# Rotated keys: one transpose per head pair and a copy to the other partitions; the last rows scaled into a tile of their own

## The chip, the cores and the metric

The kernel runs on one NeuronCore of a Trainium2 chip. The metric is device time in microseconds (us), as the median of several executions; lower is better. Five engines run their own instruction streams and wait for each other by semaphores: TensorE (PE, matrix products and transposes), VectorE (DVE), ScalarE (ACT), GpSimd (POOL) and SyncE (SP). SP issues only transfers (DMAs); ACT issues transfers between its activations, and a transfer that ACT has to wait with holds up the activations behind it.

## The reference

Two layers, each with three token mixers (a state-space scan, sliding-window attention, forgetting attention) fed by one input projection of the normalised stream, then gates, an output projection and a residual sum; at the end one RMS norm. The change touches the keys of the sliding-window mixer and the last norm:

```python
def rms_norm(x, w):
    xf = x.astype(jnp.float32)
    y = xf * lax.rsqrt(jnp.mean(xf * xf, axis=-1, keepdims=True) + NORM_EPS)
    return (y * w.astype(jnp.float32)).astype(x.dtype)

def rope(x, cos, sin):
    half = x.shape[-1] // 2
    x1, x2 = x[..., :half], x[..., half:]
    c, s = cos[None, :, None, :], sin[None, :, None, :]
    return jnp.concatenate([x1 * c - x2 * s, x2 * c + x1 * s], axis=-1)

def sliding_window_branch(q, k, v, z, sinks, cos, sin):
    ...
    q = rope(q.reshape(b, s, SWA_HEADS, HEAD_DIM), cos, sin)
    k = rope(k.reshape(b, s, SWA_KV_HEADS, HEAD_DIM), cos, sin)
    ...
    scores = jnp.einsum('bnqkgd,bnskd->bnkgqs', qb, kb).astype(jnp.float32) * (HEAD_DIM ** -0.5)
```

There are 256 tokens, a model width of 1024, 16 query heads and 4 key heads of 64 columns each. All is float32.

## The kernel before

**Products.** Each float32 product of the projections is made of three passes of a faster format: a weight piece `raw` arrives by a transfer (512 KB, L341, on SP), ACT writes its rounded part `hi` (L264), DVE the rest `lo` (L265), and PE runs hi·hi, hi·lo and lo·hi (L96). Six buffers each of `raw`, `hi` and `lo` go round: a transfer into a `raw` buffer waits until DVE has split what was in it, and ACT writes a `hi` buffer when PE has read the old one. The result of a projection stands in one of three PSUM buffers (`mm`), and the third projection after it waits until that buffer has been read.

**Order.** A planner with a clock of PE work (`pump`, `launch`, `drain`) decides at build time where the small steps of the mixers are put between the projections on PE. PE's order is kept as planned; for the other engines a scheduler orders the instructions, apart from the first three steps of layer 0, where all engines keep the planned order. Each engine then runs its list strictly in turn.

**Keys.** `u_bkv` (L476) projects the keys of 128 tokens (t = 0, 1), `rope` (L465) rotates them on DVE, and POOL adds the two halves of the rotation (L492). A score product takes queries of 64 partitions, and the queries `qT` (L522) hold two heads, one in partitions 0 to 63, the other in 64 to 127. The two heads use one key head, so that the keys are wanted in both halves. The kernel before writes each key head twice side by side (`kd`), and the transpose of that, 128x128, holds the head in both halves: four transposes on PE (L499, recorded as L100) and one activation (L500) for each t. `y.kT` holds the four heads, 256 tokens each. The first score products (`swa_quad`, L605, PE line L96 with `mx<-L,qt`) come after the first gate projection of that mixer (`u_z`, L773).

**Constants.** Ahead of the second L500 of layer 0, ACT issues the transfers of small constants of the layer (`layer_consts`, L408; they are recorded as L259): `vr`, four of `hb`, and two of `dsk`. Each `dsk` transfer brings 64x8 single elements of 4 bytes.

**Completion semaphores.** Transfers of SP and ACT use eight completion semaphores in turn, in the order in which the program has them (DMAHW0 to DMAHW7). A transfer whose semaphore was used by an earlier one that hasn't landed waits for it, on the engine that issues it.

**The end.** `out_end` (L993) adds the residual (L996, DVE), takes the sum of squares (L215, ACT), multiplies by the norm weight in place (L1001, DVE), and after the last columns works out the row factor (L1008, L226 on POOL, L228, L230) and scales the two halves of the row on DVE (L1011) and ACT (L1013), each followed by its transfer out. L1001 writes what L215 reads, and so comes after it.

Of the kernel before, what the change touches and what calls it, by code (L numbers as in the profile page):

```python
# [13 lines left out]
AF = mybir.ActivationFunctionType  # L14
ALU = mybir.AluOpType

P = 128
S = 256
D = 1024
# [6 lines left out]
D_K, D_Q, D_QK, D_G0, D_FOX, D_BDMA, D_BIAS = 6.0, 5.5, 2.0, 8.0, 0.0, 4.0, 2.0  # L26
# [17 lines left out]
def hybrid_trunk(  # L44
# [5 lines left out]
    nc = tc.nc  # L50
    x2 = x.flatten_outer_dims()
    out2 = out.flatten_outer_dims()
# [9 lines left out]
    def T(tag, shape, dtype=F32, bufs=None):  # L62
        count[0] += 1
        return sb.tile(shape, dtype, tag=tag, name=f"{tag}_{count[0]}",
                       bufs=bufs if bufs is not None else BUFS.get(tag, 1))
# [8 lines left out]
    def pmx():  # L74
        return PS("mx", 5)

    act = nc.scalar.activation
    stt = nc.vector.scalar_tensor_tensor
    tt = nc.vector.tensor_tensor
    ts = nc.vector.tensor_scalar  # L80
    gtt = nc.gpsimd.tensor_tensor
# [16 lines left out]
    def transpose(o, a, i):  # L98
        clock["t"] += 0.109
        nc.tensor.transpose(o, a, i)  # L100

    def launch(br, gen, delay=0.0):
        clock["n"] += 1
        waiting.append([clock["t"] + delay, clock["n"], br, gen, None])
# [24 lines left out]
    def pump(budget=BUDGET):  # L129
        t0 = clock["t"]  # L130
        while clock["t"] - t0 < budget:
            for m in sorted(waiting, key=lambda m: (m[0], m[1])):
                if ready(m):
                    enter(m)
                    break
            else:
                return
# [26 lines left out]
    ident = T("ident", [P, P])  # L164
# [47 lines left out]
    def sum_sq(xt, t, c, ss, n=256):  # L212

        junk = T("L2", [P, 512])
        act(junk[:, 0:n], xt[:, t, c:c + n], AF.Square, accum_out=ss)  # L215

    def row_var(ss, n):
        v = T("sm", [P, 8])
        nc.vector.tensor_reduce(v[:, 0:1], ss[:, 0:n], axis=mybir.AxisListType.X, op=ALU.add)
        ts(v[:, 0:1], v[:, 0:1], 1.0 / D, EPS, op0=ALU.mult, op1=ALU.add)  # L220
        return v
# [32 lines left out]
    def halves(ap):  # L254

        return ap.rearrange("p (a i) -> p a i", a=2)
# [142 lines left out]
    for l in range(L):  # L399
        y = Layer()  # L400
# [46 lines left out]
    def tok(ah, al, w, t, turn=True, mid=None, **kw):  # L447


        n = w.n  # L450
        p = pmm()
        b = in_turn if turn else lambda ap: ap
        if mid is None and n == 512:
            mid = pump
        dense(p[:, 0:n], lambda k: still(ah, t, k), lambda k: still(al, t, k), lambda k: b(w.hi(k)),
              lambda k: b(w.lo(k)), w, mid=mid, **kw)
        return ordered(p[:, 0:n]) if turn else p[:, 0:n]
# [7 lines left out]
    def rope(p, t):  # L465

        p4 = p.rearrange("p (h d) -> p h d", h=4)
        cos = bc(rope_sb[:, t, 0, :], 1, 4)
        a = T("L1", [P, 4, 64])
        tt(a, p4, cos, op=ALU.mult)  # L470
        b = T("L1", [P, 4, 64])
        tt(b[:, :, 0:32], p4[:, :, 32:64], bc(rope_sb[:, t, 1, 0:32], 1, 4), op=ALU.mult)
        tt(b[:, :, 32:64], p4[:, :, 0:32], bc(rope_sb[:, t, 1, 32:64], 1, 4), op=ALU.mult)  # L473
        return a, b

    def u_bkv(y, c0, t, after=None):  # L476

        def f(w):
            p = tok(y.hTh, y.hTl, w, t, turn=w.n == 512 or c0 > 0, after=after)
            if t == 0 and c0 == 0:  # L480
                kv = T("L8", [P, 2048])
                y.kT = kv[:, 0:1024].rearrange("p (h s) -> p h s", h=4)
                y.bv = kv[:, 1024:1536].rearrange("p (t c) -> p t c", t=2)
            if c0 > 0:
                act(halves(y.bv[:, t, :]), p, AF.Copy)
            elif w.n == 512:
                act(y.bv[:, t, :], p[:, 1, :], AF.Copy)
            if c0 == 0:
                a, b = rope(p if w.n == 256 else p[:, 0, :], t)
                kd = T("L2", [P, 4, 2, 64])  # L490
                for i in range(2):
                    gtt(kd[:, :, i, :], a, b, op=ALU.add)  # L492
                launch(1, rest(kd), D_K)
            pump()

        def rest(kd):
            pt = pmx()
            for h in range(4):
                transpose(pt[:, h * P:(h + 1) * P], kd[:, h, :, :].rearrange("p a b -> p (a b)"), ident)  # L499
            act(y.kT[:, :, t * P:(t + 1) * P], pt.rearrange("p (h s) -> p h s", h=4), AF.Copy)  # L500
            yield 0.0
        return f

    def u_bq(y, c0, t):
# [488 lines left out]
    def out_end(y, c, t, i, n, xo, p):  # L993
        sl = slice(c, c + n)
        with tc.high_priority():
            tt(halves(y.xn[:, t, sl]), p, halves(xo), op=ALU.add)  # L996
            sum_sq(y.xn, t, c, y.ss[t][:, i:i + 1], n)
            last = y.l + 1 == L
            nwb = fin["w"] if last else layers[y.l + 1].nwb
            if last:  # L1000
                stt(y.xn[:, t, sl], y.xn[:, t, sl], -0.5, nwb[:, sl], op0=ALU.mult, op1=ALU.mult)  # L1001
            else:
                nc.scalar.dma_start(xres[t * P:(t + 1) * P, sl], y.xn[:, t, sl])
            if i == 1:
                y.var[t] = row_var(y.ss[t], 2)
            if i == 2:
                v = y.var[t][:, 1:2]
                stt(v, y.ss[t][:, 2:3], 1.0 / D, y.var[t][:, 0:1], op0=ALU.mult, op1=ALU.add)  # L1008
                r = row_rsqrt2(v)
                if last:  # L1010
                    ts(y.xn[:, t, 0:512], y.xn[:, t, 0:512], r[:, 0:1], None, op0=ALU.mult)  # L1011
                    nc.sync.dma_start(out2[t * P:(t + 1) * P, 0:512], y.xn[:, t, 0:512])
                    act(y.xn[:, t, 512:D], y.xn[:, t, 512:D], AF.Copy, scale=r[:, 0:1])  # L1013
                    nc.scalar.dma_start(out2[t * P:(t + 1) * P, 512:D], y.xn[:, t, 512:D])
                else:
                    h = layers[y.l + 1].h[t] = T("L4", [P, D])
                    for j in range(2):
                        hs = slice(j * 512, (j + 1) * 512)
                        stt(h[:, hs], y.xn[:, t, hs], r[:, 0:1], nwb[:, hs], op0=ALU.mult, op1=ALU.mult)
        if i == 2 and not last:  # L1020
            launch(5 + t, hT(layers[y.l + 1], t), D_H[t])
        if i == 1:
            pump()

    fin = {}
# [23 lines left out]
    for y in layers:  # L1049
# [4 lines left out]
        def cols(c0, n=256):  # L1054
            return sub([(0, w[:, c0:c0 + n])], n)
# [27 lines left out]
        if l == 0:  # L1083
            k, v = cols(C_BK), cols(C_BV)
# [40 lines left out]
        o = [sub([(0, w_out[l, :, c:c + n])], n) for c, n in ((0, 256), (256, 512), (768, 256))]  # L1125
# [13 lines left out]
    with tc.manual_schedule(engines={ENG.PE, ENG.DVE, ENG.Activation, ENG.Pool}):  # L1139
# [5 lines left out]
        h = [T("L4", [P, D]) for _ in range(2)]  # L1145
# [76 lines left out]
```

## Time and profile before

| | us |
|---|---|
| runs (3) | 847.7, 848.38, 850.29 |
| median | 848.38 |
| span of the profiled execution, first to last instruction | 846.0 |
| PE busy in it | 833.7 |
| DVE, ACT, POOL busy | 642.3, 511.6, 105.7 |

The span leaves out what lies before the first instruction and after the last. The page says how long each engine was busy, which chain of work ended last, and which groups of instructions cost most; other views of the same execution list the instructions in order of time, the waits, the stretches, and the transfers with their time from issue to landing. In a row of the order of time stand its start, its length, engine, line, operation, output and inputs, shapes, and in brackets the idle time of the engine before it with what ended it; rows of equal instructions that overlap are merged, and the length is then that of all. A matmul's recorded length overlaps the next one's; the chain of waits gives what each adds.

### The profile page before, as it was taken

To read this page: it belongs to the slowest core of one execution; us is meant where nothing else is said; L and a number is where in the kernel's file an instruction comes from. 1 tells how busy PE (TensorE), PEld (TensorE's weight loads), DVE (VectorE), ACT (ScalarE), POOL (GpSimd) and SP (SyncE) were. 2 spreads that over 40 slices of the span, in tenths; PEclk is the share of its full clock that TensorE was granted. 3 is DMA by queue.
4 is the path that set the end of the run, shared out by engine and by line. 5 is a ranking of instruction groups with operands and counts; after the bars stand their busy time and mean duration, and the time that the engine had idled before them with its cause. 6 is when DMAs were issued, how large, how long until landed. Compare 5 with 4: busy or idle time off the path is not lost.

```text
span 846.0 us, 15985 instructions
## 1 busy us (share of the span) xinstructions
PE 833.7 (99%) x5964; PEld 763.4 (90%) x5964; DVE 642.3 (76%) x1403; ACT 511.6 (60%) x1004; POOL 105.7 (12%) x134
## 2 busy tenths in 40 slices
PE   8999999999999999999999999999999999999996
PEld 7989898998999998888989998899899999988896
DVE  5777997998776669656788879879968567785665
ACT  6466777665666667435555667776557667654442
POOL 6410100000140010210014001000003110121000
PEclk9999999999999999999999999999999999999999
DMA  9576565666465545748676465465755654576632
GB/s 303 160 226 197 180 199 163 197 212 184 143 188 177 181 145 189 230 147 292 206 237 218 144 204 157 145 200 182 239 172 176 174 175 152 161 236 211 212 100 76
DMA packets 126638, 158.43 MB, mean 187 GB/s; under 512 B 12784, under 2 KB 88224, under 8 KB 126560
## 3 DMA queue, kind: packets, MB, share of 16 engines
q1 hardware_dynamic: 109456, 140.79, 52.5%
q10 hardware_dynamic: 17056, 16.49, 6.3%
q8 instruction: 47, 0.77, 0.4%
q14 instruction: 31, 0.25, 0.1%
q0 software_dynamic: 48, 0.13, 0.0%
HBM read 155.22 MB, written 2.16 MB: 186 GB/s over the span
## 4 chain that ended last, share of the span: by engine, by line
PE 95%; DMA 3%; DVE 1%; ACT 0%; POOL 0%; issue 0%; SPq 0%; POOLq 0%; DVEq 0%
PE mm L96 82%; PE mx L96 9%; PE mx L100 4%; DMA raw<-in_w_in_dram 3%; DVE lo L265 0%; POOL lo L1154 0%; ACT hi L1153 0%; DVE L L470 0%; ACT L L1013 0%; DVE L L265 0%; ACT L L264 0%; POOLq L1218 0%; ACT L L215 0%; DVE L L996 0%; DVE L L1001 0%
## 5 line engine op out<-in xcount | busy, mean ns | idle before, releaser
L265 DVE TENSOR_TENSOR lo<-raw,hi 128x1024 fp32r<-128x1024 f32 x252 | 308.3, 1235 | 93.8 <-ACT hi L264 84.6
L96 PE MATMUL mm<-hi,L 128*128 128x512 f32 (+1 forms) x1344 | 373.9, 364 | 2.0 <-ACT hi L1153 1.5
L264 ACT ACTIVATE hi<-raw 128x1024 fp32r<-128x1024 f32 x252 | 263.4, 1056 | 93.5 <-PE mm L96 75.5
L96 PE MATMUL mm<-L,hi 128*128 128x256 f32 x1792 | 317.7, 278 | 0.7 <-DVE L L473 0.7
L96 PEld LDWEIGHTS mm<-L,hi 128*128 128x128 f32 x1792 | 277.7, 192 | 7.6 <-issue 3.3
L96 PEld LDWEIGHTS mm<-hi,L 128*128 128x128 f32 x1344 | 241.5, 190 | 32.5 <-issue 2.7
L96 PE MATMUL mm<-L,lo 128*128 128x256 f32 x896 | 246.4, 275 | 0.0
L96 PE MATMUL mm<-lo,L 128*128 128x512 f32 (+1 forms) x672 | 241.4, 361 | 0.6 <-POOL lo L1154 0.6
L96 PEld LDWEIGHTS mm<-L,lo 128*128 128x128 f32 x896 | 171.9, 192 | 0.2
L96 PEld LDWEIGHTS mm<-lo,L 128*128 128x128 f32 x672 | 127.3, 190 | 15.4 <-POOL lo L1154 0.8
L867 POOL TENSOR_SCALAR_AFFINE_SELECT bias<-bias 128x128 f32<-128x128 f32 x64 | 35.9, 597 | 407.5 <-DVE L L736 268.6
L561 ACT ACTIVATE pp<-pp,nm 128x128 f32<-128x128 f32 (+1 forms) x128 | 56.5, 443 | 13.5 <-DVE nm L555 13.5
L698 DVE SCALAR_TENSOR_TENSOR L<-L,vec,L 128x255 f32<-128x255 f32 (+2 forms) x96 | 46.3, 482 | 4.7 <-ACT L L695 3.4
L96 PE MATMUL mx<-L,L 128*64 128x128 f32 (+1 forms) x384 | 34.4, 314 | 0.0
L891 ACT ACTIVATE L<-L 128x512 f32<-128x512 f32 x24 | 15.1, 631 | 29.9 <-DVE L L890 29.7
L573 DVE TENSOR_SCALAR pp<-pp,rsum 128x128 f32<-128x128 f32 (+1 forms) x128 | 32.2, 316 | 0.5
L701 ACT ACTIVATE L<-L 128x256 f32<-128x256 f32 x32 | 13.3, 417 | 31.5 <-DVE L L698 25.9
L96 PEld LDWEIGHTS mx<-L,L 128*64 128x64 f32 x384 | 23.0, 136 | 9.4 <-ACT pp L561 1.3
L782 ACT ACTIVATE L<-mm 128x256 f32<-128x256 f32 x48 | 18.1, 378 | 20.8 <-PE mm L96 20.8
L590 ACT ACTIVATE L<-mx 128x512 f32<-128x512 f32 x48 | 27.0, 597 | 2.7 <-PE mx L100 2.5
L100 PE MATMUL mx<-ident,pp 128*128 128x128 f32 x192 | 26.3, 273 | 0.0
L555 DVE CUSTOM_DVE_ANT_0 pp<-mx,wmask,nsink 128x128 f32<-128x128 f32 x64 | 23.4, 412 | 1.5 <-PE mx L96 1.5
(173 smaller groups left out, 717.5 us busy)
## 6 DMA issues: line engine op xcount, KB each, us to landing
raw<-in_w_in_dram SPq DMA_DIRECT2D x200, 512.0 KB, 4.5
raw<-in_w_proj_dram SPq DMA_DIRECT2D x48, 512.0 KB, 5.5
raw<-in_w_out_dram SPq DMA_DIRECT2D x16, 512.0 KB, 4.6
L<-cumd ACTq DMA_DIRECT2D x8, 512.0 KB, 5.0
bias<-cumd ACTq DMA_DIRECT2D x16, 256.0 KB, 4.0
L<-in_gate_bias_dram ACTq DMA_DIRECT2D x12, 256.0 KB, 3.9
L<-in_x_dram SPq DMA_DIRECT2D x2, 512.0 KB, 4.9
nwb<-in_norm_w_dram SPq DMA_DIRECT2D x1, 512.0 KB, 5.3
```

The source lines that it names most:

```text
L96: nc.tensor.matmul(o, a, b, **kw)
L100: nc.tensor.transpose(o, a, i)
L264: keep(act)(hi, src, AF.Copy)
L265: keep(tt)(lo, src, hi.bitcast(F32), op=ALU.subtract)
L555: nc.vector.tensor_tensor_reduce(out=pp[:, i, sl], in0=score(p, i, b), in1=biases(p, i, b), scale=-0.125, scalar=1.0e30 if ns is None else ...
L561: act(pp[:, i, sl], pp[:, i, sl], AF.Exp, scale=-1.0, bias=nm[:, e:e + 1], accum_out=sums[:, e:e + 1])
L573: ts(pp[:, i, sl], pp[:, i, sl], rs[:, 2 * i + b:2 * i + b + 1], 0.5, op0=ALU.mult, op1=ALU.mult)
L590: act(pT, pt, AF.Copy)
L698: stt(a[:, s:S], x_[:, 0:S - s], y.vec[:, 16 * j + u:16 * j + u + 1], a[:, s:S], op0=ALU.mult, op1=ALU.add)
L782: act(halves(th), p, AF.Tanh, scale=0.5)
L867: nc.gpsimd.affine_select(out=bias[:, i, dst], in_=bias[:, i, src], compare_op=ALU.is_ge, fill=NEG, base=0, pattern=[[-1, P]], channel_mul ...
L891: act(g, g, AF.Tanh, scale=0.5)
```

## The change

For each t the keys are rotated into a tile `k` of four heads side by side, with one addition on POOL. Two transposes on PE, each of a pair of heads, give the even heads in partitions 0 to 63 and the odd ones in 64 to 127. Two activations of 64 partitions put them into `y.kT`. After t = 1 two transfers issued by ACT copy the even heads to partitions 64 to 127 and the odd ones to 0 to 63: 64 partitions, 2 heads, 256 tokens, 128 KB each. In the last layer the product with the norm weight goes into a new tile `fin["y"]` in place of `y.xn`, and the row factor and the transfers out work on that tile.

```diff
             if c0 == 0:
                 a, b = rope(p if w.n == 256 else p[:, 0, :], t)
-                kd = T("L2", [P, 4, 2, 64])
+                k = T("L1", [P, 4, 64])
+                gtt(k, a, b, op=ALU.add)
+                launch(1, rest(k.rearrange("p h d -> p (h d)")), D_K)
+            pump()
+
+        def rest(k):
+            pt = pmx()
+            for j in range(2):
+                transpose(pt[:, j * P:(j + 1) * P], k[:, j * P:(j + 1) * P], ident)
+            k2 = y.kT.rearrange("p (j i) s -> p j i s", i=2)
+            for i in range(2):
+                r = slice(64 * i, 64 * i + 64)
+                act(k2[r, :, i, t * P:(t + 1) * P], pt[r, 0:2 * P].rearrange("p (j s) -> p j s", j=2), AF.Copy)
+            yield 0.0
+            if t == 1:
                 for i in range(2):
-                    gtt(kd[:, :, i, :], a, b, op=ALU.add)
-                launch(1, rest(kd), D_K)
-            pump()
-
-        def rest(kd):
-            pt = pmx()
-            for h in range(4):
-                transpose(pt[:, h * P:(h + 1) * P], kd[:, h, :, :].rearrange("p a b -> p (a b)"), ident)
-            act(y.kT[:, :, t * P:(t + 1) * P], pt.rearrange("p (h s) -> p h s", h=4), AF.Copy)
-            yield 0.0
+                    nc.scalar.dma_start(k2[64 - 64 * i:128 - 64 * i, :, i, :], k2[64 * i:64 * i + 64, :, i, :])
...
             if last:
-                stt(y.xn[:, t, sl], y.xn[:, t, sl], -0.5, nwb[:, sl], op0=ALU.mult, op1=ALU.mult)
+                if i == 0 and t == 0:
+                    fin["y"] = T("L8", [P, 2, D])
+                stt(fin["y"][:, t, sl], y.xn[:, t, sl], -0.5, nwb[:, sl], op0=ALU.mult, op1=ALU.mult)
...
                 if last:
-                    ts(y.xn[:, t, 0:512], y.xn[:, t, 0:512], r[:, 0:1], None, op0=ALU.mult)
-                    nc.sync.dma_start(out2[t * P:(t + 1) * P, 0:512], y.xn[:, t, 0:512])
-                    act(y.xn[:, t, 512:D], y.xn[:, t, 512:D], AF.Copy, scale=r[:, 0:1])
-                    nc.scalar.dma_start(out2[t * P:(t + 1) * P, 512:D], y.xn[:, t, 512:D])
+                    o = fin["y"]
+                    ts(o[:, t, 0:512], o[:, t, 0:512], r[:, 0:1], None, op0=ALU.mult)
+                    nc.sync.dma_start(out2[t * P:(t + 1) * P, 0:512], o[:, t, 0:512])
+                    act(o[:, t, 512:D], o[:, t, 512:D], AF.Copy, scale=r[:, 0:1])
+                    nc.scalar.dma_start(out2[t * P:(t + 1) * P, 512:D], o[:, t, 512:D])
```

**How it moves instructions.** First ACT in layer 0, around the second step of the keys, where the constants are issued; `hi_491` and `hi_503` before (`hi_489` and `hi_501` after) are the last two pieces of the second query projection, which PE takes up at 39.76 us of the profile before. Before:

```order
L259 DMA hb_405<-in_a_log_dram 128x16
L259 DMA dsk_410<-in_d_skip_dram 64x8x1 x2
L500 ACTIVATE L_50_265<-mx_426 128x4x128
L264 ACTIVATE hi_491<-raw_319 128x1024
L264 ACTIVATE hi_503<-raw_325 128x1024
```

With the change:

```order
L259 DMA hb_402<-in_a_log_dram 128x16
L259 DMA dsk_407<-in_d_skip_dram 64x8x1 x2
L502 ACTIVATE L_50_265<-mx_423 64x2x128 x2
L506 DMA L_50_265<-L_50_265 64x2x256 x2
L264 ACTIVATE hi_489<-raw_317 128x1024
L264 ACTIVATE hi_501<-raw_323 128x1024
```

The two copies stand directly behind the two `dsk` transfers in ACT's list, and ahead of the two `hi` pieces.

Second SP in layer 0: the weight pieces issued from about 33 us on, with the semaphores that each waits for (DVE: the `raw` buffer must be split; a completion semaphore: an earlier transfer must have landed). The two copies take two completion semaphores in between, so that the pieces behind them get other ones. Before:

```order
L341 DMA raw_495<-in_w_in_dram 128x4x256 [waits DMAHW4_49,DMAHW2_49,DVE_49]
L341 DMA raw_507<-in_w_in_dram 128x4x256 [waits DMAHW7_49,DMAHW6_49,DVE_49]
L341 DMA raw_590<-in_w_in_dram 128x4x256 [waits DMAHW7_49,DMAHW0_49,DVE_49]
L341 DMA raw_596<-in_w_in_dram 128x4x256 [waits DMAHW1_49,DMAHW0_49,DVE_49]
L341 DMA raw_608<-in_w_in_dram 128x4x256 [waits DMAHW1_49,DVE_49]
L341 DMA raw_620<-in_w_in_dram 128x4x256 [waits DMAHW2_49,DVE_49]
```

With the change:

```order
L341 DMA raw_493<-in_w_in_dram 128x4x256 [waits DMAHW4_49,DMAHW2_49,DVE_49]
L341 DMA raw_505<-in_w_in_dram 128x4x256 [waits DMAHW7_49,DMAHW0_49,DVE_49]
L341 DMA raw_588<-in_w_in_dram 128x4x256 [waits DMAHW1_49,DVE_49]
L341 DMA raw_594<-in_w_in_dram 128x4x256 [waits DMAHW2_49,DVE_49]
L341 DMA raw_606<-in_w_in_dram 128x4x256 [waits DMAHW3_49,DVE_49]
L341 DMA raw_618<-in_w_in_dram 128x4x256 [waits DMAHW6_49,DMAHW4_49,DVE_49]
```

Semaphore 2 belongs to the first row in both. Before, the sixth row waited for it; with the change the fourth does, two transfers earlier.

Third DVE at the end, the last 256 columns of the second 128 rows, with what each instruction waits for. Before:

```order
L996 TENSOR_TENSOR L_1975_10131<-mm_10332,L_2007_10330 128x256 [waits PE_49]
L1001 SCALAR_TENSOR_TENSOR L_1975_10131<-L_1975_10131,nwb_9781 128x256 [waits Activation_49]
L1008 SCALAR_TENSOR_TENSOR sm_10327<-ss_10134,sm_10327 128x1
L228 SCALAR_TENSOR_TENSOR sm_10364<-sm_10362,sm_10327 128x1 [waits Pool_49]
```

With the change:

```order
L1001 TENSOR_TENSOR L_1975_10127<-mm_10329,L_2008_10327 128x256 [waits PE_49]
L1008 SCALAR_TENSOR_TENSOR L_1988_10203<-L_1975_10127,nwb_9777 128x256 [waits DVE_49]
L1015 SCALAR_TENSOR_TENSOR sm_10324<-ss_10130,sm_10324 128x1 [waits Activation_49]
L228 SCALAR_TENSOR_TENSOR sm_10361<-sm_10359,sm_10324 128x1 [waits Pool_49]
```

The product with the norm weight (L1001 before, L1008 now) no longer waits for ACT's sum of squares; the first step of the row factor does.

On PE nothing moves but the transposes of the keys, two in place of four at each of four places, and in layer 1 the next transposes a few products apart. In layer 1 ACT and DVE also split the 64-column piece of the small projection (128x8x32) two weight pieces earlier than before.

## The prediction

> **What bounds the kernel now.** First the page, then the waits of PE, then the chain of waits between 20 and 60 us, where the keys of layer 0 are made.
>
> ```profile
> PE 833.7 (99%) x5964; PEld 763.4 (90%) x5964; DVE 642.3 (76%) x1403; ACT 511.6 (60%) x1004; POOL 105.7 (12%) x134
> PE 95%; DMA 3%; DVE 1%; ACT 0%; POOL 0%; issue 0%; SPq 0%; POOLq 0%; DVEq 0%
> ```
>
> PE is busy for 99% of the span and is 95% of the chain: an edit is worth what it takes from PE's list, or from the few places where PE stands. The waits of PE from 30 to 840 us, the longest (in total, times, longest one):
>
> ```profile
> PE mm L96 <- DVE L L473: 0.7, 1, 0.7
> ```
>
> That one wait is what matters here. The chain (start, length, what):
>
> ```profile
> 25.74 0.44 PE mx L100 x4
> ...
> 28.77 0.44 PE mx L100 x4
> ...
> 36.82 15.02 DMA raw<-in_w_in_dram
> ...
> 55.40 2.95 PE mm L96 x24
> ```
>
> The two L100 rows are the key transposes of layer 0. Behind them the chain leaves PE: a weight piece that SP begins to issue at 36.82 takes 15.0 us to land, and PE goes on at 55.40 only after what hangs on it. Why 15 us is told by stretches and two groups of transfers:
>
> ```profile
> 36.00:40.00 4.00, 4.00 (x22) 3.52 (x21) 4.00 (x7) 1.81 (x3) 1.27 (x1) 1.00 0.05 0
> 40.00:44.00 4.00, 4.00 (x23) 3.50 (x22) 1.81 (x9) 1.15 (x4) 1.44 (x3) 1.00 0.04 0
> 44.00:46.00 2.00, 2.00 (x11) 1.76 (x10) 1.00 (x3) 1.06 (x1) 1.13 (x2) 1.00 0.56 183
> 46.00:50.00 4.00, 4.00 (x30) 3.68 (x29) 1.14 (x2) 1.07 (x1) 0.00 (x0) 1.00 1.09 360
> ```
>
> ```profile
> L259 ACTq DMA_DIRECT2D dsk<-in_d_skip_dram x2: 646/646/646, 31.5 to 32.2; - x2
> DMA to landing us min/median/max: 9.8/9.8/9.8
> ```
>
> ```profile
> L341 SPq DMA_DIRECT2D raw<-in_w_in_dram x1: 368/368/368, 33.7 to 33.7; - x1
> DMA to landing us min/median/max: 14.5/14.5/14.5
> ```
>
> The last two numbers of a stretch are the share of the DMA engines and GB/s. From 36 to 44 nothing but the single elements of `dsk` moves; the first landed 9.8 us after its issue, and the piece issued at 33.7, behind them, at 48.2. From 44 the backlog of pieces runs, at 360 GB/s from 46. The keys' copies are issued into this jam.
>
> The wait it causes, in order of time:
>
> ```profile
> 51.94 1.07 ACT L264 ACTIVATE hi<-raw 128x1024 fp32r<-128x1024 f32 x1 [0.45 <-DMA raw<-in_w_in_dram]
> 53.09 1.58 PE L96 MATMUL mx<-L,qt 64*128 64x128 f32 x16
> 53.40 1.21 DVE L265 TENSOR_TENSOR lo<-raw,hi 128x1024 fp32r<-128x1024 f32 x1
> 54.53 0.42 DVE L470 TENSOR_TENSOR L<-mm,rope 128x256 f32<-128x256 f32 x1
> 55.40 0.38 PE L96 MATMUL mm<-L,hi 128*128 128x256 f32 x1 [0.73 <-DVE L L473]
> ```
>
> A piece lands, ACT and DVE split it, and only behind that in DVE's list comes the rotation that frees the PSUM buffer. PE ends the score products (second row) at 54.67 and stands 0.73 us.
>
> **The change part by part.** The sum is made on the span of 846.0; the median of the runs lies 2.4 above it, and I carry these 2.4 along.
>
> *Transposes.* Four are 0.44 us in the chain, so two of four save 0.22 at each of four places, 0.44 in each layer. In layer 0 PE comes 0.44 earlier to the wait at 55.40, which a transfer ends: nothing is gained, the wait becomes 1.17. In layer 1 PE is not short of work after 437 until 839, so that 0.44 counts. If the wait at 55.40 were absent, both would.
>
> *The copies in layer 0.* They are 2 x 128 KB, issued after the piece of 33.7 and before the next. If they only share the way, the pieces behind them come later by 0.26 MB at 360 GB/s: 0.73 us. If they stand ahead of the backlog until `dsk` is through, the 183 GB/s x 2 us = 0.37 MB that the pieces moved between 44 and 46 are put off as well: 1.0 + 0.73 = 1.75. If they fill gaps, nothing. A gain isn't seen: what jams the queue is issued before them. The trace has no copy from partitions to partitions; I take 0.73, as the stretch of 46 to 50 is where they would run. PE then goes on at 56.13, so +0.73 for layer 0.
>
> The Trainium skill, SBUF — State Buffer, "Door 1: The DMA port swizzle", says that 64 partitions reach only half of the memory's DMA ports, so half the rate; by that the copies would be put at an estimated 1.5 us and the sum 0.7 higher. No row here shows a transfer to 64 partitions of any size.
>
> *Edits costed at nothing.* Score products need the copies at 53.09 - 0.44 = 52.65; a piece issued just before them lands at 48.2, so 4 us cover them, and beyond that each us costs one. ACT now reads each transposed pair in two activations and issues two transfers:
>
> ```profile
> 32.85 0.60 ACT L500 ACTIVATE L<-mx 128x512 f32<-128x512 f32 x1 [4.46 <-DMA hb<-in_dt_bias_dram]
> 33.34 1.99 ACT L264 ACTIVATE hi<-raw 128x1024 fp32r<-128x1024 f32 x2
> 34.43 3.50 DVE L265 TENSOR_TENSOR lo<-raw,hi 128x1024 fp32r<-128x1024 f32 x3 [1.04 <-ACT hi L264]
> 39.76 0.68 PE L96 MATMUL mm<-hi,L 128*128 128x512 f32 x2
> ```
>
> ```profile
> L522 ACT ACTIVATE qt<-mx x4: 381/382/383, 39.8 to 43.1; 128x256 f32<-128x256 f32 x4
> ...
> L341 SPq DMA_DIRECT2D raw<-in_w_in_dram x24: 367/368/569, 407.1 to 465.4; - x24
> ...
> DMA to landing us min/median/max: 3.4/4.9/7.3
> ```
>
> An activation of 256 columns takes 0.38 (L522, 128 partitions), so two are 0.2 more than the 0.60 of L500; two issues at the 0.65 of `dsk` are 1.3. The `hi` pieces behind them come 1.5 later; their `lo` is done at about 35.7 now and PE takes up the piece at 39.76 - 0.44 = 39.3: 3.6 us of cover, 2.1 left. The fourth piece on SP waits with the change for the transfer that lands at 48.2; before, the wait lay two transfers later. Two pieces, 1 MB or 2.9 us of backlog, stand ahead of it, and a piece lands 3.4 us after its issue at the least, 1.4 of it its own 0.5 MB, so the stream has no hole. POOL loses four additions, which were hidden: no wait of PE after 30 us is for POOL. The new tile's buffer is an old one long read. In layer 1:
>
> ```profile
> L341 SPq DMA_DIRECT2D L<-in_w_in_dram x2: 447/1364/2282, 431.7 to 432.2; - x2
> DMA to landing us min/median/max: 7.2/7.2/7.3
> ```
>
> ```profile
> 437.89 1.06 ACT L264 ACTIVATE hi<-raw 128x1024 fp32r<-128x1024 f32 x1 [1.52 <-PE mm L96]
> ...
> 438.98 2.51 DVE L265 TENSOR_TENSOR lo<-raw,hi 128x1024 fp32r<-128x1024 f32 x2 [1.78 <-ACT hi L264]
> ...
> 444.91 0.29 PE L96 MATMUL mm<-hi,L 128*128 128x256 f32 x1
> ```
>
> The small piece lands at 439.4, and its split now stands behind the `hi` of 437.89: the pieces after it come about 1 us later, and PE takes them up behind the product of 444.91, so that some 4 us cover them; without that cover it would cost that 1 us. The copies of layer 1 come behind no `dsk`, and the planner puts the first scores well behind them.
>
> *The end.*
>
> ```profile
> 839.61 0.52 ACT L L215 x2
> ...
> 840.15 0.42 DVE L L1001
> 840.58 0.08 DVE sm L1008
> ```
>
> L1001 moves beside L215: 0.42 off the chain, less at most 0.1 if L1008 already overlaps it.
>
> Sum: +0.73 - 0.44 - 0.42 = -0.1: a span of 845.9, a time of **848.3**.
>
> **The rivals.** *A, the forecast*: 0 to 1.75 for the copies, so 847.5 to 849.3. For it: every term has its row.
>
> *B, the gain is kept.* The jam of 31 to 46 us ends a little sooner, since POOL, with two additions fewer, disturbs DVE less while it splits the pieces (DVE's pieces took 1.2 us alone), or the copies fill gaps: the wait at 55.40 keeps its 0.73 or loses it, and both 0.44 count in part. -0.44 - 0.42 gives 847.5, with the whole wait and both savings 846.3. Against it: the constants, not DVE, set the jam.
>
> *C, slower: ACT stands at the issue of the copies.*
>
> ```profile
> 36.82 4.97 SPq L341 DMA_DIRECT2D raw<-in_w_in_dram  x1
> ```
>
> SP's third piece behind `dsk` took 4.97 us to issue, to 41.79. ACT's copies are third and fourth behind `dsk` in ACT's own queue. If ACT stands as long, `hi` starts at 41.8, ends at 42.9, `lo` at 44.2; PE would begin the piece at 43.8 instead of 39.76, 4.0 late, which swallows the wait of 0.73: +3.3 - 0.44 - 0.42 gives 850.8. If ACT stands until the backlog runs at full rate (46), 855.0. It decides from an issue that ends after about 37, and makes the kernel slower by a measurable amount from about 42. Against it: `dsk` itself was issued in 0.65 behind four `hb`.
>
> *D, slower: the copies land late.* Behind `dsk` in the same queue, they could get their turn only when the backlog of SP's pieces ends; the piece issued at 52.8 landed 6.5 later, at 59.3:
>
> ```profile
> L341 SPq DMA_DIRECT2D raw<-in_w_in_dram x1: 368/368/368, 52.8 to 52.8; - x1
> DMA to landing us min/median/max: 6.5/6.5/6.5
> ```
>
> The scores would begin 6.2 late, less 0.73: 848.4 + 5.5 - 0.86 = 853.0. It decides from 52.65. Against it: in layer 1 a transfer that ACT issued 7 us after `dsk` landed 10.1 us later, among SP's pieces, not behind them.
>
> ```profile
> L887 ACTq DMA_DIRECT2D L<-in_gate_bias_dram x1: 334/334/334, 371.5 to 371.5; - x1
> DMA to landing us min/median/max: 10.1/10.1/10.1
> ```
>
> **How the numbers follow.** The measurable bound is 0.3%, 2.5 us (below 845.8, above 850.9). A 0.45, all within it. B 0.14, of which 0.06 falls below by the runs' own spread (847.7 to 850.3). C 0.27, 0.21 beyond and 0.06 within. D 0.14, beyond. So faster 0.06, same 0.59, slower 0.35. A alone is 847.2 to 849.6 with the spread; reaching into B, C and D until about 0.2 is left out, the range is 846.9 to 853.2.
>
> **What would show it.** Right: in layer 0 ACT's two issues under 1 us each; the `hi` behind them near 35; PE's first score products near 52.7 without a wait, then one wait of 1 to 2 us on the rotation near 55; two L100 transposes at each of four places; at the end the product with the norm weight beside the sum of squares, 0.4 less from PE's last matmul to the end. Wrong: an issue of several us on ACT before 42 (C); score products that wait for the copies (D); or a new wait of PE for a split piece in layer 1.

## The result and the profile after

| | before | changed |
|---|---|---|
| median of 11 runs, us | 847.81 | 853.84 |
| lowest to highest | 847.25 to 850.29 | 848.67 to 858.0 |
| span of the profiled execution | 846.0 | 851.4 |

The ratio is 1.0064, with an interval of 1.0047 to 1.0081: slower by 6 us. The spread is part of the result: the runs before lie within 3 us here (in the later groups four of 107 lie above 852, one at 853.74), those of the changed kernel within 9, two of them (848.67, 850.09) near the old time.

The page of the changed kernel (engines, then the chain by engine and by line):

```profile
PE 834.4 (98%) x5956; PEld 762.2 (90%) x5956; DVE 640.8 (75%) x1403; ACT 512.8 (60%) x1008; POOL 101.9 (12%) x130
PE 92%; DMA 3%; issue 1%; ACTq 1%; DVE 1%; ACT 1%; POOL 0%; SPq 0%; POOLq 0%; DVEq 0%
PE mm L96 79%; PE mx L96 9%; PE mx L100 4%; DMA raw<-in_w_in_dram 2%; DMA raw<-in_w_proj_dram 1%; ACTq L506 1%; ACT hi L264 0%; DVE lo L265 0%; POOL lo L1162 0%; POOL L L518 0%; ACT hi L1161 0%; DVE L L265 0%; DVE L L470 0%; ACT L L1021 0%;
```

PE falls from 95% to 92% of the chain, and a new name stands in it: ACTq L506, ACT's sequencer at the issue of the key copies. The waits of PE from 30 to 60 us, where before there was one, 0.7 on the rotation:

```profile
PE mm L96 <- ACT hi L264: 3.3, 1, 3.3
PE mm L96 <- DVE lo L265: 0.6, 1, 0.6
PE mx L100 <- POOL L L518: 0.4, 1, 0.4
```

ACT in order of time in the same stretch (L502 puts the transposed keys into `y.kT`, L506 is the copies):

```profile
31.16 1.36 ACTq L259 DMA_DIRECT2D dsk<-in_d_skip_dram  x2
32.56 0.78 ACT L502 ACTIVATE L<-mx 64x256 f32<-64x256 f32 x2 [4.47 <-PE mm L96]
34.43 6.61 ACTq L506 DMA_DIRECT2D L<-L  x2
41.14 3.90 ACT L264 ACTIVATE hi<-raw 128x1024 fp32r<-128x1024 f32 x4 [7.80 <-issue]
```

The two copies take 6.61 us to issue. Four `hi` pieces, of which the first began at 33.34 before, stand behind them and begin at 41.14, 7.80 later than in the old kernel. The chain of waits shows what led to that and what became of it (start, length, what):

```profile
27.51 6.85 DMA raw<-in_w_in_dram
...
34.43 0.63 ACTq L506
...
35.15 5.89 ACTq L506
...
41.14 1.06 ACT hi L264
...
43.37 0.79 DVE lo L265
...
45.24 1.21 DVE lo L265
...
47.33 1.58 POOL L L518
...
48.95 0.69 PE mx L100 x2
```

ACT is done with L502 at 33.34, and the first copy goes out only at 34.43: the chain puts that 1.0 down to a weight piece that landed at 34.36, whose completion semaphore the copy takes next. The first copy went out in 0.63, the second held ACT for 5.89. That is not a wait for a completion semaphore, which is a row of its own ahead of it, of 0.02 at 35.10. Behind it the chain doesn't return to PE with the first piece: it runs through ACT, DVE's `lo` and rotations and POOL's addition to the second query transposes at 48.95. For the size, PE's list around these transposes. Before:

```profile
42.43 0.60 PE L100 MATMUL mx<-ident,L 128*128 128x128 f32 x4
42.79 0.68 PE L96 MATMUL mm<-hi,L 128*128 128x512 f32 x2
```

With the change:

```profile
48.95 0.69 PE L100 MATMUL mx<-ident,L 128*128 128x128 f32 x2 [0.38 <-POOL L L518]
49.29 0.89 PE L96 MATMUL mm<-hi,L 128*128 128x512 f32 x2
```

The product behind them starts 6.50 later. The wait of 0.73 on the rotation is gone, layer 1 saves the 0.44 that was forecast (its transposes are pairs of 0.22 in the chain), and the end saves 0.34, as shown below: 6.50 - 0.73 - 0.44 - 0.34 = 5.0. The spans differ by 5.4; 0.3 of the rest is found at the very end.

One more thing is new. Stretches of the changed kernel (busy time of PE, PEld, DVE, ACT, POOL; granted clock of PE, share of the DMA engines, GB/s):

```profile
42.00:44.00 2.00, 1.19 (x3) 0.79 (x4) 1.77 (x2) 2.00 (x4) 0.00 (x0) 0.72 0.04 0
44.00:46.00 2.00, 2.00 (x6) 1.53 (x6) 2.00 (x5) 1.70 (x4) 0.54 (x1) 0.50 0.77 256
46.00:48.00 2.00, 2.00 (x7) 1.42 (x6) 2.00 (x5) 0.00 (x0) 1.71 (x2) 0.50 1.17 260
48.00:50.00 2.00, 1.62 (x7) 1.18 (x6) 1.77 (x7) 0.71 (x2) 1.71 (x3) 0.57 1.05 305
```

After its stand PE runs at half its clock from about 43 until 49.7. Half a clock over some 6 us looks like 3 us lost, and a reader of PE's rows alone would put them on the bill beside the 3.31 of the stand. The experiments ask whether that is so.

At the end the product with the norm weight moved as it should. The last 256 columns, before:

```profile
839.61 0.42 ACT L215 ACTIVATE L<-L 128x256 f32<-128x256 f32 x1 [1.69 <-DVE L L996]
840.15 0.42 DVE L1001 SCALAR_TENSOR_TENSOR L<-L,nwb 128x256 f32<-128x256 f32 x1 [0.57 <-ACT L L215]
840.49 0.15 DVE L1008 SCALAR_TENSOR_TENSOR sm<-ss,sm 128x1 f32<-128x1 f32 x1
```

With the change:

```profile
845.04 0.42 ACT L215 ACTIVATE L<-L 128x256 f32<-128x256 f32 x1 [1.69 <-DVE L L1001]
845.04 0.42 DVE L1008 SCALAR_TENSOR_TENSOR L<-L,nwb 128x256 f32<-128x256 f32 x1
845.58 0.16 DVE L1015 SCALAR_TENSOR_TENSOR sm<-ss,sm 128x1 f32<-128x1 f32 x1
```

From the start of the sum of squares to the first step of the row factor it is 0.88 before, 0.54 after: 0.34 less. Most of this is given back behind it. From the start of ACT's last scaling to the end of the span it is 4.2 us before (841.83 to 846.0) and 4.5 after (846.93 to 851.4). The 4.5 stands in the profile of every kernel below in which SP or ACT issues the copies and `dsk` comes in single elements, with the new end or the old one; the 4.2 stands in tail_only, without copies, and in pool_copies, where POOL issues them. So the copies cost these 0.3 us; by what path was not tried.

### The profile page after: what moved, and what is told of

The parts are those of the page before. It is cut to its first block, busy times and chain, and to the rows that moved or that the text cites. A ratio compares the mean times of both kernels' runs of the same rounds, so it can differ in the third digit from the quotient of the medians.

```text
span 851.4 us, 15977 instructions
## 1 busy us (share of the span) xinstructions
PE 834.4 (98%) x5956; PEld 762.2 (90%) x5956; DVE 640.8 (75%) x1403; ACT 512.8 (60%) x1008; POOL 101.9 (12%) x130
## 4 chain that ended last, share of the span: by engine, by line
PE 92%; DMA 3%; issue 1%; ACTq 1%; DVE 1%; ACT 1%; POOL 0%; SPq 0%; POOLq 0%; DVEq 0%
PE mm L96 79%; PE mx L96 9%; PE mx L100 4%; DMA raw<-in_w_in_dram 2%; DMA raw<-in_w_proj_dram 1%; ACTq L506 1%; ACT hi L264 0%; DVE lo L265 0%; POOL lo L1162 0%; POOL L L518 0%; ACT hi L1161 0%; DVE L L265 0%; DVE L L470 0%; ACT L L1021 0%; DVE L L945 0%
```

## The experiments

All are compared with the kernel before on the same chip, whose median was 847.6 to 847.9 in each group.

### Which part of the change: keys_only, tail_only, before_copies

keys_only is the changed kernel with the old end.

> Leaves out the change at the end (the last rows are scaled in place as before). Theory: in layer 0 the second copy's issue holds ACT from about 35 to 41 us behind the single elements of dsk in ACT's own queue, the two hi pieces behind it come late, PE stands some 3.3 us and then runs at half clock for some 6 us; all of the loss is there. So the same shape here, ACT's issue 5 to 7 us long, and a median of 851 to 857, some 0.3 above the changed kernel or equal to it. Rival, the end costs the time: 847 to 849.

tail_only is the kernel before with the new end.

> The kernel before with the change at the end alone. Theory: 0.33 to 0.42 less from PE's last product to the end, 847.3. Rival, the new tile or its transfers give it back: 847.7 or more. The interval may not tell these apart; the rows from PE's last product on do.

before_copies adds the copies and nothing else:

```diff
             act(y.kT[:, :, t * P:(t + 1) * P], pt.rearrange("p (h s) -> p h s", h=4), AF.Copy)
             yield 0.0
+            k2 = y.kT.rearrange("p (j i) s -> p j i s", i=2)
+            if t == 1:
+                for i in range(2):
+                    nc.scalar.dma_start(k2[64 - 64 * i:128 - 64 * i, :, i, :], k2[64 * i:64 * i + 64, :, i, :])
```

> The kernel before with nothing but the two copies added per layer, issued by ACT at the place where the change issues them; they copy key heads onto themselves (both halves hold them already), with four transposes as before and the old end. Theory: the copies' place in ACT's list alone makes the loss, so two kinds of executions, some near 848 and most at 852 to 856, median 852 to 855. Rival, the halves' activations, the fewer transposes or their order make it: 847.5 to 849.5.

Measured: keys_only 853.56, ratio 1.0052 (1.0030 to 1.0074); tail_only 847.52, 0.9999 (0.9987 to 1.0011); before_copies 854.79, 1.0081 (1.0062 to 1.0100), all six runs from 854.03 to 856.2. The new end shows no loss, and the copies alone make all of the loss. In before_copies ACT's rows are those of the changed kernel:

```profile
35.03 6.80 ACTq L505 DMA_DIRECT2D L<-L  x2
41.94 3.90 ACT L264 ACTIVATE hi<-raw 128x1024 fp32r<-128x1024 f32 x4 [8.86 <-issue]
```

The ten runs of keys_only are of two kinds, 848.27 and 848.52, and eight from 852.47 to 854.48, and the profiled execution is one of the two. The same two places in it, ACT's list and the chain:

```profile
34.14 1.34 ACTq L506 DMA_DIRECT2D L<-L  x2
35.58 3.91 ACT L264 ACTIVATE hi<-raw 128x1024 fp32r<-128x1024 f32 x4 [1.93 <-issue]
```

```profile
43.40 0.44 PE mx L100 x2
```

The same program, the same order, but the copies went out in 1.34, and the time is that of the kernel before: what is lost is lost at this issue. after_2 is another profiled execution of the changed kernel, to see whether the time goes with this issue:

> The changed kernel again for its profile alone. Theory: its time follows the length of ACT's second issue: near 6 us with 853 to 857, under 1 us with 848 to 849.

It took 853.97, with the second copy at ACT's sequencer for 6.13 us:

```profile
36.11 6.13 ACTq L506
...
50.15 0.44 PE mx L100 x2
```

What differs ahead of the short and the long issue is SP: in this execution of keys_only a weight piece was issued at 31.61, between the two `dsk` transfers (31.41, 32.18); in the two profiles of the changed kernel and in that of before_copies it came behind both (32.49, with `dsk` at 31.16 and 31.88, in the first). The other profiles fit, on SP or on ACT: where the piece was issued 0.55 us or more after the start of the second `dsk`, an issue is held for 4.97 to 6.13; where it was issued at most 0.25 after it, for 3.08 or less. That is an order seen in thirteen profiles, and no kernel varied it by itself.

### What holds the issue: sp_copies, pool_copies, dsk_late, dsk_rows

sp_copies and pool_copies let another engine issue the copies (`nc.sync` or `nc.gpsimd` in place of `nc.scalar`).

> The changed kernel with the copies issued by SP (in both layers), behind the second piece after dsk. Theory: SP stands instead of ACT, where SP's third piece stood 4.97 before anyway; the weight pieces behind come up to 1.5 later, so hi near 33.5, no stand at 42, a wait near 55 of 0.7 to 2.5: 847 to 849.5. Rival, the copies in flight disturb the pieces, whoever issues them: 853 or more.

> The changed kernel with the copies issued by POOL (in both layers) in place of ACT, at the same place in the order; POOL has no work there until 38 us. Theory: what costs is that ACT's hi pieces stand behind the issue; with POOL issuing, hi starts near 33.5 and PE has no stand at 42: 847 to 849. If POOL stands at the issue until 41, its addition for the queries (38.7 before) comes 2 to 4 late and PE waits for it: 849 to 851. Rival, the copies in flight at that time disturb the pieces, whoever issues them: 853 or more.

sp_copies 848.30, 1.0007 (0.9997 to 1.0017); pool_copies 848.58, 1.0017 (1.0006 to 1.0028). With SP the second copy is held too, for 2.06 us, but what stands behind it is a weight piece that had time:

```profile
34.98 2.06 SPq L506 DMA_DIRECT2D L<-L  x1
```

PE has no wait at 42 in either profile, with SP's copies one of 0.5 near 55, with POOL's one of 0.6 for POOL's addition. Both profiles are of the fastest of twelve executions (846.23, 846.86); it is the medians that carry the reading. So the copies in flight disturb nothing worth 6 us. It matters who stands.

dsk_late turns the order round in layer 0, copies first (`load_dsk` holds the two `dsk` transfers, which `layer_consts` now issues in layer 1 alone):

```diff
...
+                if y.l == 0:
+                    load_dsk(y)
```

> The changed kernel, but in layer 0 ACT issues the two dsk transfers behind the two copies in place of ahead of them. Theory: both copies are issued in about 0.65 each and land 3 to 5 us after their issue, the hi pieces start near 36, PE has no stand at 42; the jam comes 1 to 3 us later, so the wait on the rotation near 55 is between 0 and 2. Median 846.5 to 849. Rival, the copies by themselves take long to issue (64 partitions): ACT stands at the second one as in the changed kernel, 853 to 855. Second rival, dsk then holds ACT by its own second issue: the hi pieces late again, 851 or more.

dsk_rows brings `d_skip` as rows of 16 numbers, as the `hb` vectors come:

```diff
-        for half in range(2):
-            src = d_skip[l:l + 1, :].rearrange("o (j two) -> two o j", two=2)[half]
-            pdma(y.dsk[64 * half:64 * half + 64, :], src.to_broadcast([64, NK]))
+        y.drow = T("drow", [P, 2 * NK], bufs=2)
+        pdma(y.drow, d_skip[l:l + 1, :].to_broadcast([P, 2 * NK]))
...
+        dr = y.drow.rearrange("p (j two) -> p two j", two=2)
+        for half in range(2):
+            r = slice(64 * half, 64 * half + 64)
+            pin(ts)(y.dsk[r, :], dr[r, half, :], 1.0, None, op0=ALU.mult)
```

> The changed kernel, but d_skip is loaded as whole rows of 16 numbers to 128 partitions, as the hb vectors are, and two small DVE instructions pick the single columns of dsk (both layers). Theory: no transfers of single elements, so no empty stretch from 36 to 44 us, the copies land 3 to 5 us after their issue, no wait of PE on the rotation near 55 (0.73 before), and the savings of the change show: 847.8 - 0.7 - 0.9 - 0.3 = 845.9. Rival, the copies by themselves hold ACT: 853. Rival, the jam is the backlog of the weight pieces and stays without dsk: 847 to 848 with the wait of 0.7.

dsk_late 850.06, 1.0020 (1.0002 to 1.0038); dsk_rows 847.16, 0.9991 (0.9978 to 1.0003). ACT in dsk_late:

```profile
32.23 1.39 ACTq L511 DMA_DIRECT2D L<-L  x2
35.47 1.31 ACTq L259 DMA_DIRECT2D dsk<-in_d_skip_dram  x2
36.89 3.91 ACT L264 ACTIVATE hi<-raw 128x1024 fp32r<-128x1024 f32 x4 [4.28 <-PE mm L96]
```

With `dsk` behind them the copies are issued in 1.39: 64 partitions aren't slow by themselves, and layer 1's copies say the same (1.30 for both in the changed kernel). Without single elements the 6 us don't come either. In both kernels PE still waits near 43, and for POOL. dsk_late:

```profile
PE mx L100 <- POOL L L525: 2.2, 2, 1.4
```

dsk_rows:

```profile
PE mx L100 <- POOL L L521: 1.6, 2, 1.0
```

I had expected no wait there, and both times lie above what I expected (846.5 to 849, and 845.9). The reason shows when the start of the `hi` pieces is put beside that of the later of the two pairs of query transposes:

| | hi begins | transposes | difference |
|---|---|---|---|
| dsk_rows | 35.45 | 43.55 | 8.10 |
| keys_only | 35.58 | 43.40 | 7.82 |
| dsk_late | 36.89 | 44.70 | 7.81 |
| changed kernel | 41.14 | 48.95 | 7.81 |
| before_copies | 41.94 | 50.03 | 8.09 |
| after_2 | 42.34 | 50.15 | 7.81 |

Seen from the moment at which ACT is free, ACT, DVE and POOL take 7.8 to 8.1 to the transposes, whatever PE does. In the kernel before `hi` began at 33.34, so this path was ready at 41.2 to 41.4 (POOL's addition ended at 41.39 there) and PE came at 42.43: **1.0 to 1.3 us of cover**. Two issues of the ordinary sort, 1.3 us, and the wait of one of them for a weight piece that has its completion semaphore use it up: without a hold ACT stood so for 0.4 in keys_only and for 1.9 in dsk_rows, and in dsk_late for 1.8 ahead of `dsk`. A held issue goes through the cover whole.

### Is the half clock paid for? fill28, copies_fill

fill28 gives PE work where it stood in the changed kernel, products that nobody reads:

```diff
+            if y.l == 0 and c == 1 and t == 0:
+                for _ in range(28):
+                    nc.tensor.matmul(pt[:, 256:512], y.hTh[:, 0, 0, 0:P], y.hTh[:, 0, 0, :], start=True, stop=True)
```

> The changed kernel with 28 more products of 128x256 on PE (their result is not used), put behind the query transposes after which PE stood from 38.9 to 42.3 us: 28 x 0.11 = 3.1 us of work that nobody needs. Theory: PE's clock was halved because PE stood; with PE busy the granted clock stays at 1.00 from 42 to 50 us, and the 6.4 us at half clock are worth 3.2, so the time falls from 853.8 to about 850.6, although PE has more to do. Rival, the clock falls for another reason (the late pieces, the transfers): the clock row stays at 0.50, and the time is 853.8 or up to 3 more.

fill28: 853.30, 1.0057 (1.0038 to 1.0075). The mean clock of its runs is 0.995 to 0.999, where that of the changed kernel's is 0.991 to 0.999, and the time is the same. But its runs were of two kinds (five from 850.24 to 851.01, seven from 853.07 to 856.96), and the profiled execution had a hold of 3.08 only. copies_fill therefore fills before_copies, with 30 products.

> before_copies (the kernel before with the copies alone, where all six timed executions were at 854.0 to 856.2) with 30 products of 128x256 on PE, of no use, 3.3 us of work, in the place where PE stood for 3.77. If the half clock after the stand is part of the loss, the clock stays at 1.00 from 43 to 48 us and the time falls by what the half clock cost there, 3 to 4 us at half speed, 1.5 to 2 us: 852.9. If the loss is the chain of ACT's hi, DVE's lo and rotations and POOL's addition, which starts when ACT's issue ends, the clock stays at 1.00 and the time doesn't move: 854.5 to 855.5, PE waits for POOL longer near 49.

> copies_fill again for its profile alone, since the first profile fell on an execution with a short hold of ACT (2.5 us). If the hold is the long one (6 us): the chain goes through ACT's hi, DVE and POOL to the query transposes near 50 us whatever the clock (the loss is the chain), or PE is busy through to 55 and what it does is the bound (then the filling itself is paid).

> A third profile of copies_fill, for the same: with a long hold of ACT (6 us) either the chain through ACT's hi, DVE and POOL sets the transposes near 50 us with the clock at 1.00, or PE's own work does.

copies_fill: 857.09, 1.0106 (1.0086 to 1.0126). In the first two profiled executions (851.74 and 850.98) the hold was short, 2.51 and 2.18; in the third, of 857.01, it was 5.65. In this third: PE's wait for POOL from 30 to 60 us, the stretches, the start of the `hi` pieces, and the transposes:

```profile
PE mx L100 <- POOL L L517: 2.9, 2, 2.3
```

```profile
44.00:46.00 2.00, 1.44 (x9) 1.00 (x8) 1.58 (x2) 2.00 (x3) 0.00 (x0) 1.00 0.12 22
46.00:48.00 2.00, 2.00 (x10) 1.51 (x8) 2.00 (x3) 1.77 (x4) 0.00 (x0) 1.00 1.01 290
48.00:50.00 2.00, 0.12 (x1) 0.00 (x0) 2.00 (x5) 0.00 (x0) 1.28 (x1) 1.00 1.10 229
```

```profile
43.33 3.90 ACT L264 ACTIVATE hi<-raw 128x1024 fp32r<-128x1024 f32 x4 [8.58 <-issue]
```

```profile
51.42 0.44 PE L100 MATMUL mx<-ident,L 128*128 128x128 f32 x2 [0.58 <-POOL L L517]
```

The long stand of PE is filled, the clock stays at 1.00, and PE at full speed only waits for POOL instead: 2.9 us, and the transposes come 8.09 after `hi`, as in before_copies. The table above says the same of the changed kernel: 7.81 at half clock, 7.82 in keys_only at full clock. The half clock of the changed kernel is real and costs little, since PE wasn't what the time hung on. What can be charged to it is the last pair of transposes, 0.69 in place of 0.44 in the chain, and the 24 products behind them, 5.28 in place of 5.18 in keys_only. That copies_fill as a whole is 2.3 slower than before_copies, and above both of my forecasts, is not settled: in its third profile ACT's issue ended at 43.22, in that of before_copies at 41.83, since the constants themselves were issued later (`dsk` at 32.76, 31.09 there).

### Without the hold: late_copies, late_copies_rows, before_dsk_rows, before_tail_rows

late_copies issues layer 0's copies behind the four query activations, with ACT's order held (at the old place they are issued in layer 1 alone):

```diff
...
             act(qT[:, :, t * P:(t + 1) * P], pt[:, 0:256].rearrange("p (h s) -> p h s", h=2), AF.Copy)
+            if y.l == 0 and c == 1 and t == 1:
+                k2 = y.kT.rearrange("p (j i) s -> p j i s", i=2)
+                for i in range(2):
+                    pdma(k2[64 - 64 * i:128 - 64 * i, :, i, :], k2[64 * i:64 * i + 64, :, i, :])
```

> The changed kernel, but in layer 0 ACT issues the two copies behind the four query activations, about 43 us, ten places later in its list; dsk stays as it is. Theory: the hi pieces start again near 33.5, PE has no wait from 38 to 50 us, the wait on the rotation near 55 is 0.5 to 2, and the savings show: 846.5 to 848.3 with little spread. Rival, it is the copies in the jam and not ACT's list: ACT stands at them again, later, or the first scores wait for them: 850 or more.

> As late_copies, and d_skip is loaded as rows as in dsk_rows. Theory: neither a wait from 38 to 50 (1.56 us in dsk_rows) nor the wait on the rotation near 55 (0.73 before), so the savings are added to both: 847.8 - 0.73 - 0.88 - 0.33 = 845.9. Rival, what is saved there comes back at the next wait, since the weight stream is the bound up to 60 us: 847, as dsk_rows.

> The kernel before with d_skip loaded as rows and nothing else. Theory: the empty stretch of transfers from 36 to 44 us is made by dsk's single elements; without them the wait on the rotation at 55.40 goes, 847.8 - 0.7 = 847.1. Rival, the stretch stays without dsk (the pieces wait for something else): no change, 847.8.

before_tail_rows adds the new end to before_dsk_rows.

> The kernel before with the change at the end and d_skip loaded as rows, keys as before. Theory: 846.1 (measured with rows alone) - 0.35 = 845.8; then 845.24 with the keys of the change behind the query activations leaves 0.5 to 0.6 for the transposes (0.88 worked out from the chain). Rival, the change of the keys brings nothing: 845.2 here too.

| | median | ratio | interval | lowest to highest |
|---|---|---|---|---|
| late_copies | 848.07 | 1.0003 | 0.9992 to 1.0015 | 846.86 to 850.58 |
| late_copies_rows | 845.24 | 0.9967 | 0.9957 to 0.9978 | 844.94 to 846.7 |
| before_dsk_rows | 846.12 | 0.9977 | 0.9964 to 0.9989 | 845.97 to 846.47 |
| before_tail_rows | 845.78 | 0.9972 | 0.9961 to 0.9984 | 845.71 to 846.45 |

late_copies has the old time again: no wait from 38 to 50, and near 55 the old one:

```profile
PE mm L96 <- DVE L L473: 0.6, 1, 0.6
```

In late_copies_rows PE's chain from 30 to 60 us names nothing but PE, and ACT issues the copies in 0.68 and 0.60:

```profile
38.53 0.44 PE mx L100 x4
38.97 2.59 PE mm L96 x12
41.56 0.44 PE mx L100 x4
41.99 5.18 PE mm L96 x24
```

late_copies_rows beats both kernels, by 2.4 us over the one before. Most of that is `dsk`: before_dsk_rows, the old kernel without its single elements, is 1.5 faster, twice what I expected, and its twelve runs lie within 0.5 us where the old ones lie within 5.8. In before_dsk_rows the empty stretch is gone (36 to 40 us, 0 GB/s before):

```profile
36.00:40.00 4.00, 4.00 (x23) 3.50 (x22) 3.93 (x9) 1.81 (x4) 1.64 (x1) 1.00 0.96 294
```

The second half of the 1.5 has a candidate. Layer 1's constants bring `dsk` too, near 365 us, and in four profiles with single elements PE stands for 0.5 to 0.8 near 387, behind a late piece: in tail_only a weight piece of that time took 12.66 us to land,

```profile
369.77 12.66 DMA raw<-in_w_proj_dram
...
387.24 0.66 PE mx L100 x4
```

and PE stood for 0.59 ahead of these transposes. The profiles of the four kernels with rows have no such wait. That it makes up the rest wasn't tried by itself. The change's own part is then small: late_copies_rows and before_tail_rows are 0.5 apart, and their intervals overlap. The end alone, before_tail_rows against before_dsk_rows, is worth 0.34 again, but these two come from different groups.

## Why the prediction was wrong

I forecast 848.3 with no measurable change; the kernel is slower, at 853.84, above the range by 0.6. (The forecast stood on the median of three runs, 848.38; over eleven it is 847.81.) It went by rival C, which had 0.27, and at a higher price than C had (850.8). The step that failed stands among the edits costed at nothing: two issues on ACT at 1.3 us, `hi` 1.5 later, 2.1 of cover left. Measured are 6.5 us for the two issues, a wait of 1.0 ahead of them, `hi` 7.80 later, and a cover of about 1.

**The sentence that failed first** is the one against C: "`dsk` itself was issued in 0.65 behind four `hb`". It counted ACT's queue alone and compared with `hb`, whose elements are rows. What had to be counted is what is issued behind `dsk`, over both engines. In the old profile, two of SP's pieces go through behind `dsk` and the third is held, for 4.97, to 41.79, half a microsecond after the first `dsk` landed. With the change one piece of SP's and ACT's first copy go through, and the third, ACT's second copy, is held for 5.89, to 41.04. The row that carried C was on the table with nearly the right number; I put it down to SP. The Trainium skill, DMA: Bandwidth & Descriptors, "Issuing engines are not separate DMA queues", says that transfers run on the same 16 DMA engines whichever engine issues them; the runs fit that: the third issue was held whether it was SP's or ACT's, 4.97 and 5.89 us. The page adds that the time an issue takes is usually small beside the transfer; here it was up to 6.13 of the 13.7 us from the start of the issue to the landing (after_2).

**The wait ahead of the first copy: at nothing.** The prediction followed the completion semaphores on SP, and not on ACT. The two copies take two of them as well, and the first stood 1.0 for a weight piece.

**Cover, "3.6 us of cover, 2.1 left": wrong.** It was taken from the moment at which PE takes the piece. Between the pieces in DVE's list stand rotations, and behind those POOL's additions of 0.7 to 1.6, and PE's query transposes hang on them. By that path the cover was 1.0 to 1.3, and 0.6 to 0.9 once the 0.44 that the prediction took off is taken off here too. The 1.5 of extra ACT work that it counted is more than that; no run had this work alone. In dsk_rows, with no hold at all, PE waits 1.6 there, but ACT's stand of 1.9 for a weight piece is part of it. I named who waits for `hi` and stopped one engine short.

**C's price, +3.3 net of the wait: too low by 2.5;** 6.50 - 0.73 = 5.8. C let PE start 4.0 late and go on at its own speed. The pieces come one at a time from ACT and DVE, with rotations between, and the product behind the second transposes came 6.50 late.

**Delay of the weight pieces, +0.73: not seen as a longer wait.** Where ACT isn't held, PE waits near 55 for 0.6 (late_copies) or 0.5 (sp_copies), where the two kernels without copies had 0.73 (before) and 0.38 (tail_only).

**Transposes: right** in layer 1, -0.44. In layer 0 they were to be swallowed by the wait at 55.40; that wait was overtaken by the loss.

**The end: right at its place, 0.34 for 0.42;** the 0.1 that the prediction held back for the overlap of L1008 is what is missing. In tail_only the runs can't tell it from nothing (0.9987 to 1.0011), and in the changed kernel the 0.3 that the copies add behind it were in no term.

**D: it didn't come about.** The copies landed at 48.1 and 49.0, and the first scores came at 59.8, late themselves. **B: its idea was near.** The constants do set the jam, and with rows in place of elements and the copies issued later the kernel is faster, but nothing in this change touches the constants.

**The clock** was in no part of the prediction. Had it been foreseen and charged to C at some 3 us, the sum would have been 853.8, right by accident.

## What to carry to other kernels

A transfer in an engine's list is an instruction that can hold what stands behind it: ahead of adding one, look for a held issue in the trace of before, on any engine, and count the new issue among those behind the same jam. Look on the issuing engine too for the transfer that has the new one's completion semaphore. Follow cover through every list that the late work feeds, to the engine that sets the time, and not to the first place where that engine meets the work. A transfer of single elements is worth removing even where nobody waits for its own data: here two of 2 KB in each layer made most of the spread of the old kernel, 5.8 us against 0.5 without them.

## What the runs showed of the hardware

- Behind two `dsk` transfers (64x8 elements of 4 bytes each) the third further issue of SP and ACT was held for 4.97 to 6.13 us in layer 0, whether SP's (4.97 before, 5.63 in tail_only) or ACT's (5.89 in the changed kernel, 6.13 in after_2 and before_copies, 5.65 in the third copies_fill), until 0.5 to 1.8 us after the first `dsk` had landed. Where SP's piece was issued ahead of the second `dsk` or at most 0.25 us after its start, the hold was between nothing (keys_only) and 3.08 (fill28). What is full there, the runs don't say.
- PE's granted clock fell to 0.50 after stands of 3.3, 3.8 and 4.0 us and was back at 1.00 3.4 to 6.8 us later; a stand of 2.3 left it at 1.00 (copies_fill, third profile), and with the long stand filled it stayed at 1.00. The Trainium skill, TensorE: Matmul & The Clock Gate, "What's actually happening", gives half rate after an idle window of about 3.4 us; the trace agrees in the rate and nearly in the length (3.31 idle, 0.50). In none of these kernels did it change the end of the path by more than 0.4.
- Copies of 128 KB between partition halves that weren't held were issued in 0.6 to 0.7 us each by ACT and landed, in layer 1, 3.3 us after the issue at the least in the changed kernel and 2.4 in keys_only. No run compared them with copies of 128 partitions.
